# The state recurrence of a chunked linear attention: from a chain of updates to prefix scans, and a prologue with part of its constants made later

## The chip, the cores and the metric

The kernel runs on one core of a Trainium2 chip. The metric is the device time of one execution in microseconds (us), from the first to the last instruction and what lies around them. A core has five engines with an instruction queue each: the matrix engine (PE), the vector engine (DVE), the scalar engine (ACT), GpSimd (POOL) and SyncE (SP, which here only issues DMA transfers). Each engine works its own queue in order, and semaphores hold an instruction until what it needs is there.

## The reference, cut to what matters

The program is two layers of a hybrid network over 1152 tokens (128 of a prompt, 1024 of a sample; the two groups are independent sequences). In each layer a normalised and modulated input is projected to 2336 columns, which feed a windowed attention with a sink, a gated linear attention (GLA), and a gated linear recurrence (RG-LRU); an output projection and a feed-forward block of width 4096 follow. The GLA has four heads of width 64 and two directions, and works in chunks of 64 tokens:

```
b = jnp.cumsum(g, axis=2)                    # within a chunk
q_in = q * jnp.exp(b);  k_in = k * jnp.exp(-b);  k_end = k * jnp.exp(b_last - b)
o_intra = causal(q_in k_in^T) v
delta = jnp.einsum('bnchd,bnchv->bnhdv', k_end, v)
decay = jnp.exp(b_last[:, :, 0])
s[c + 1] = decay[c][:, None] * s[c] + delta[c]      # over the chunks
o = o_intra + q_in s[c]
```

So a state of 64 x 64 numbers runs over 2 chunks of the prompt (from zero) and over 16 of the sample (from a given state), forwards, and in the other direction backwards. The final states of the prompt are outputs.

## The kernel before

Every array is held with channels on the partitions and 1152 tokens along the free dimension, in three blocks (`tb`) of 384 tokens. A product in full precision is three products of split numbers (`dense`, L155 to L157), twelve of which make a tick.

PE's order is written out by hand: `tick` advances generators that sit in `self.chain`, one step for every twelve projection products, so that small PE work is strewn between the projections. The other engines get their order from a scheduler that goes by its own cost estimates and the order in the program.

**The GLA, `gla_pair`.** Two heads make a pair; a layer has two pairs. A head has its forward direction on partitions 0 to 63 and its backward direction on 64 to 127. `cum` makes the running sums of the gate (two scans over half the partitions each, L595 and L596). Then come six steps (two heads, three blocks). `pre` of a step subtracts the running sum from its value at the chunk's end (L634 on DVE for the forward half, L635 on POOL for the backward half), takes the exponential (L636, ACT) and multiplies the key (L637, DVE); `trans` transposes this on PE (L643) and copies it out (L645, ACT); `delta`, one step later, multiplies it with the values (L653, PE), copies the six 64 x 64 results out of PSUM (L654, ACT) and makes the scaled queries and keys with two exponentials (L659, L662, ACT) and two products (L660, L663, POOL). After a head's third block `states` runs the recurrence: 34 instructions `upd` (L672, DVE), one for each chunk and direction, each over 64 partitions and 64 columns. A generator spreads them over the following ticks. The states land in `Sc`, chunk by chunk.

Then `intra` multiplies queries with keys (L718), masks (L720) and adds the directions (L724); `outer` adds the contributions of values (L732) and states (L738) in one PSUM bank; `headsum` and `gate` normalise and gate the output.

**The prologue.** `run` loads and transposes the inputs, sums their squares, and makes each token's scale. While the modulation matrix streams in (`mod_round`, L249), `scaled` multiplies the three blocks with the scale (`spread`, L329, and L369, half on POOL and half on DVE). When the modulation is there (`mod_fin`, L257 to L282, which yields the gains G), `norm1_first` finishes each block: gain and shift (L380 on ACT, L382 on DVE), the high part (L383, ACT), the low part (L385). `vecs` makes the constants of a layer; its last 27 DVE instructions (L198 to L222) serve the RG-LRU and the gate alone.

Of the kernel before, what the change touches and what calls it, by code (L numbers as in the profile page):

```python
# [28 lines left out]
PPOS = 11  # L29
V_BMOD, V_N1, V_N2, V_CW, V_CB, V_GN, V_BA, V_BX, V_LAM, V_SL, V_GB, V_FN, V_C, V_CC = (  # L30
# [8 lines left out]
def blk(t, tb):  # L39
    return t[:, tb * TB:(tb + 1) * TB]  # L40
# [8 lines left out]
class Net:  # L49
# [111 lines left out]
    def vecs(self, l):  # L161
# [25 lines left out]
        if l == 0:  # L187
# [7 lines left out]
            self.cs = cs  # L195
        hb = self.const.tile([128, 8], F32, name=f"hb{l}")
# [160 lines left out]
    def scaled(self, tb, rs):  # L357
        nc = self.nc
        g = self.spread(rs, lambda: self.np.tile([128, TB], F32, tag="pb", name="pb", bufs=3))
# [6 lines left out]
        for kt, path in enumerate('pvpvpvpv'):  # L366
            t = self.np.tile([128, TB], F32, tag="nt", name="nt", bufs=24)
            eng = nc.gpsimd if path == "p" else nc.vector
            eng.tensor_tensor(t, self.xa(kt, tb), pbs, ALU.mult)  # L369
            ts.append(t)  # L370
        return ts

    def norm1_first(self, tb, ts):
# [12 lines left out]
        self.spill(tb)  # L386
        yield
# [42 lines left out]
    def mixer(self, l):  # L430
# [131 lines left out]
        def gla_pair(pair, hook):  # L562
# [49 lines left out]
            def start(hf):  # L612
                Bt, qd, kd = H[hf]
                Bc = Bt.rearrange("p (c s) -> p c s", s=64)
                dec = gp.tile([128, 18], F32, tag="dec", name="dec", bufs=2)
                nc.scalar.activation(dec[0:64], Bc[0:64, :, 63], AF.Exp, scale=-1.0 / 16)
                nc.scalar.activation(dec[64:128], Bc[64:128, :, 0], AF.Exp, scale=-1.0 / 16)
                dl, S = B(), B()
                Sc = S.rearrange("p (c v) -> p c v", v=64)
                nc.gpsimd.memset(Sc[0:64, 0], 0.0)  # L620
                nc.gpsimd.memset(Sc[64:128, 1], 0.0)
                nc.sync.dma_start(Sc[0:64, 2], I["state_gla"][0, l, 0, 2 * pair + hf])
                nc.sync.dma_start(Sc[64:128, 17], I["state_gla"][0, l, 1, 2 * pair + hf])
                st[hf] = (dec, dl, Sc, B())

            def pre(hf, tb):
# [3 lines left out]
                Bc = Bt.rearrange("p (c s) -> p c s", s=64)  # L630
# [16 lines left out]

            def delta(hf, tb, kn):
                Bt, qd, kd = H[hf]
                dec, dl, Sc, kin = st[hf]  # L650
# [6 lines left out]
                b = blk(Bt, tb)  # L657
                e = tg()
                nc.scalar.activation(e, b, AF.Exp, scale=-1.0 / 16)  # L659
                nc.gpsimd.tensor_tensor(blk(qd, tb), blk(qd, tb), e, ALU.mult)  # L660
                e = tg()
                nc.scalar.activation(e, b, AF.Exp, scale=1.0 / 16)  # L662
                nc.gpsimd.tensor_tensor(blk(kin, tb), blk(kd, tb), e, ALU.mult)  # L663

            def states(hf):
                dec, dl, Sc, kin = st[hf]
# [860 lines left out]
```

## Time and profile before

| | us |
|---|---|
| median of 3 runs (2927.18 to 2929.66) | 2928.68 |
| the profiled execution, its own time | 2926.49 |
| span of the profiled execution | 2924.7 |

The span is what the trace covers. A share in a window is busy time over its length. PEclk is the clock that PE was granted, as a share of 2.4 GHz. "Idle before" names what ended an engine's idle time.

### The profile page before, as it was taken

What the parts mean: (1) busy time and instruction counts of PE and PEld (TensorE: products, weight loads), DVE (VectorE), ACT (ScalarE), POOL (GpSimd) and SP (SyncE); (2) the same over time, 40 slices, a digit from 0 to 9 for tenths busy, and PEclk for the clock granted to TensorE, in tenths of its full rate; (3) what the DMA queues carried; (4) which work ended last, traced back from release to release, by engine and by line L of the source; (5) the groups of instructions that cost most, each with busy time, mean ns of one, the idle gap of its engine ahead of it and who ended that gap; (6) DMA issues with size and microseconds to landing.
All of it is one profiled execution on the core that took longest, in us unless ns stands there. A gap on an engine that the chain in (4) does not pass through costs nothing.

```text
span 2924.7 us, 41719 instructions
## 1 busy us (share of the span) xinstructions
PE 2749.6 (94%) x16067; PEld 2621.1 (90%) x16067; DVE 1540.2 (53%) x2818; ACT 1062.2 (36%) x1957; POOL 807.7 (28%) x843
## 2 busy tenths in 40 slices
PE   5897988999999999999987989899899999999998
PEld 3787987889999999999987879888899999999998
DVE  7668577785332333233478577777832332233235
ACT  4424447764112112211354325477622112211223
POOL 5323446752001001100223234576311001100112
PEclk7998999999999999999999999999999999999999
DMA  7535338421321111111333643662211111111113
GB/s 261 134 106 156 113 127 265 143 73 58 101 80 44 44 44 37 44 44 44 107 105 88 175 131 101 200 218 75 70 46 44 44 37 43 44 44 44 40 41 130
DMA packets 279303, 273.66 MB, mean 94 GB/s; under 512 B 30032, under 2 KB 259008, under 8 KB 279104
## 3 DMA queue, kind: packets, MB, share of 16 engines
q1 hardware_dynamic: 278888, 270.92, 30.3%
q8 instruction: 127, 2.08, 0.3%
q14 instruction: 72, 0.59, 0.1%
q10 hardware_dynamic: 216, 0.06, 0.0%
HBM read 227.02 MB, written 43.91 MB: 93 GB/s over the span
## 4 chain that ended last, share of the span: by engine, by line
PE 63%; DVE 7%; ACT 2%; issue 2%; POOL 1%; DMA 1%; SPq 0%; POOLq 0%; DVEq 0%; ACTq 0%
PE pg L156 18%; PE pg L155 18%; PE pg L157 18%; DVE B L672 1%; PE pd L155 1%; PE pg L1098 1%; PE pd L156 1%; PE pd L157 1%; PE pg L1066 1%; DVE tn L343 1%; PE pe L249 1%; PE pd L1204 1%; PE pd L1205 1%; PE pd L1206 1%; PE pg L1089 1%
## 5 line engine op out<-in xcount | busy, mean ns | idle before, releaser
L118 ACT CAST wh<-wr 128x1024 fp32r<-128x1024 f32 x228 | 239.0, 1048 | 918.2 <-PE pg L156 826.1
L156 PE MATMUL pg<-hl,wh 128*128 128x384 f32 x1584 | 538.4, 340 | 2.6 <-DVE hl L345 1.5
L155 PE MATMUL pg<-hh,wh 128*128 128x384 f32 x1584 | 538.6, 340 | 1.8 <-ACT hh L344 1.8
L157 PE MATMUL pg<-hh,wl 128*128 128x384 f32 x1584 | 536.9, 339 | 0.0
L1247 POOL TENSOR_TENSOR te<-te 128x384 f32<-128x384 f32 x192 | 166.5, 867 | 1330.3 <-ACT uh L1246 1329.4
L155 PE MATMUL pg<-uh,wh 128*128 128x384 f32 x1536 | 515.1, 335 | 0.6 <-ACT wh L118 0.6
L157 PE MATMUL pg<-uh,wl 128*128 128x384 f32 x1536 | 514.1, 335 | 1.7 <-DVE wl L119 1.7
L156 PE MATMUL pg<-ul,wh 128*128 128x384 f32 x1536 | 513.8, 334 | 0.0
L1269 DVE SCALAR_TENSOR_TENSOR x<-pg,mod,x 128x384 f32<-128x384 f32 (+2 forms) x512 | 254.3, 515 | 396.3 <-PE pg L157 396.2
L119 DVE TENSOR_TENSOR wl<-wr,wh 128x1024 fp32r<-128x1024 f32 x196 | 244.9, 1250 | 191.1 <-ACT wh L118 190.9
L1248 DVE TENSOR_TENSOR ul<-te,uh 128x384 fp32r<-128x384 f32 x192 | 107.1, 558 | 451.1 <-POOL te L1247 451.1
L155 PE MATMUL pd<-hh,wh 128*128 128x384 f32 x816 | 295.1, 362 | 25.1 <-DVE te L480 9.5
L155 PEld LDWEIGHTS pg<-hh,wh 128*128 128x128 f32 x1584 | 299.2, 189 | 5.4 <-issue 3.4
L156 PEld LDWEIGHTS pg<-hl,wh 128*128 128x128 f32 x1584 | 299.3, 189 | 5.0 <-DVE hl L351 2.4
L157 PEld LDWEIGHTS pg<-hh,wl 128*128 128x128 f32 x1584 | 299.2, 189 | 0.0
L155 PEld LDWEIGHTS pg<-uh,wh 128*128 128x128 f32 x1536 | 288.9, 188 | 4.3 <-issue 1.7
L157 PEld LDWEIGHTS pg<-uh,wl 128*128 128x128 f32 x1536 | 288.7, 188 | 2.1 <-DVE wl L119 2.0
L156 PEld LDWEIGHTS pg<-ul,wh 128*128 128x128 f32 x1536 | 288.9, 188 | 0.0
L156 PE MATMUL pd<-hl,wh 128*128 128x384 f32 x816 | 283.9, 348 | 3.3 <-DVE hl L385 3.3
L157 PE MATMUL pd<-hh,wl 128*128 128x384 f32 x816 | 283.3, 347 | 0.0
L1245 ACT ACTIVATE te<-pg 128x384 f32<-128x384 f32 x192 | 93.8, 489 | 357.7 <-PE pg L157 357.7
L155 PEld LDWEIGHTS pd<-hh,wh 128*128 128x128 f32 x816 | 160.9, 197 | 34.7 <-DVE te L480 10.8
(273 smaller groups left out, 4373.3 us busy)
## 6 DMA issues: line engine op xcount, KB each, us to landing
wr<-in_w_mlp_dram SPq DMA_DIRECT2D x144, 512.0 KB
wm<-in_w_mod_dram SPq DMA_DIRECT2D x96, 512.0 KB
wr<-in_w_out_dram SPq DMA_DIRECT2D x48, 512.0 KB
wr<-in_w_in_dram SPq DMA_DIRECT2D x36, 512.0 KB
xd<-x SPq DMA_DIRECT2D x48, 192.0 KB
x<-xd SPq DMA_DIRECT2D x48, 192.0 KB
raw<-mixd SPq DMA_DIRECT2D x40, 192.0 KB
B<-gkd SPq DMA_DIRECT2D x16, 288.0 KB
```

The costliest lines, as they stand in the source:

```text
L118: nc.scalar.copy(hi[:, :m], raw[:, :m])
L119: lo_eng.tensor_tensor(lo[:, :m], raw[:, :m], f32(hi[:, :m]), ALU.subtract)
L155: mm(out, wh[i], xs[i][0], start=i == 0, stop=False)
L156: mm(out, wh[i], xs[i][1], start=False, stop=False)
L157: mm(out, wl[i], xs[i][0], start=False, stop=i == n - 1)
L249: nc.tensor.matmul(p[32 * g:32 * g + 32, :], self.cs[:, kt, :], ws[g // 2][:, 512 * (g % 2):512 * (g % 2) + 512], start=kt == 0, stop=kt = ...
L343: nc.vector.scalar_tensor_tensor(t[:, a:b], x(kt, tb)[:, a:b], G()[:, kt, s:s + 1], pbs[:, a:b], ALU.mult, ALU.mult)
L672: nc.vector.scalar_tensor_tensor(out, Sc[r, c], dec[r, c:c + 1], dc[r, c], ALU.mult, ALU.add)
L1245: nc.scalar.activation(r, p[:, :TB], AF.Relu)
L1247: nc.gpsimd.tensor_tensor(r, r, r, ALU.mult)
L1248: nc.vector.tensor_tensor(blk(ul, tb), r, f32(blk(uh, tb)), ALU.subtract)
L1269: nc.vector.scalar_tensor_tensor(xa, p[:, a:b], self.M[l]["g2"][:, dt, s:s + 1], xa, ALU.mult, ALU.add)
```

## The change

The recurrence of a head becomes four prefix scans. A new tile `dl` holds, for each of the 64 value columns, a row of NP = 19 places: a zero, the two chunks of the prompt, the start state, and the chunks of the sample (the backward direction in reverse order, so that both directions run the same way). The decays lie in a row of the same 19 places, with zeros at the places where a new sequence starts, and are repeated 16 times (`dr`), so that one scan over 304 numbers does 16 value columns. `delta` writes its results into this order, at a step of 19 numbers, with one copy for each direction (in the first block, which has both sequences, two for each). `states` runs the scans in place, and four copies, two on ACT and two on POOL, bring the states back into chunk order in `Sc`. `pre` uses the copied chunk-end values `bl` for both directions, in one DVE instruction. There is one `dl` for all heads; `dec` has one buffer. Temporaries move from `tg` (8 to 5 buffers) to `tn` (6).

In the prologue only two blocks go through `scaled` and `norm1_first`. The third goes through the ordinary `norm`, in pieces during the first projections, and the 27 late constants are made behind it (`vecs_late`).

```diff
+NP = 19
...
+        if l:
+            self.vecs_late(l)
+
+    def vecs_late(self, l):
+        nc, V = self.nc, self.V[l]
+        vt = V["vt"]
         hb = self.const.tile([128, 8], F32, name=f"hb{l}")
...
-        g = self.spread(rs, lambda: self.np.tile([128, TB], F32, tag="pb", name="pb", bufs=3))
+        g = self.spread(rs, lambda: self.np.tile([128, TB], F32, tag="pb", name="pb", bufs=2))
...
-            t = self.np.tile([128, TB], F32, tag="nt", name="nt", bufs=24)
+            t = self.np.tile([128, TB], F32, tag="nt", name="nt", bufs=16)
...
+    def late(self, l):
+        self.vecs_late(l)
         yield
...
             def start(hf):
                 Bt, qd, kd = H[hf]
                 Bc = Bt.rearrange("p (c s) -> p c s", s=64)
-                dec = gp.tile([128, 18], F32, tag="dec", name="dec", bufs=2)
-                nc.scalar.activation(dec[0:64], Bc[0:64, :, 63], AF.Exp, scale=-1.0 / 16)
-                nc.scalar.activation(dec[64:128], Bc[64:128, :, 0], AF.Exp, scale=-1.0 / 16)
-                dl, S = B(), B()
-                Sc = S.rearrange("p (c v) -> p c v", v=64)
-                nc.gpsimd.memset(Sc[0:64, 0], 0.0)
-                nc.gpsimd.memset(Sc[64:128, 1], 0.0)
-                nc.sync.dma_start(Sc[0:64, 2], I["state_gla"][0, l, 0, 2 * pair + hf])
-                nc.sync.dma_start(Sc[64:128, 17], I["state_gla"][0, l, 1, 2 * pair + hf])
-                st[hf] = (dec, dl, Sc, B())
+                dec = gp.tile([128, NP], F32, tag="dec", name="dec", bufs=1)
+                nc.gpsimd.memset(dec, 0.0)
+                bl = gp.tile([128, 18], F32, tag="bl", name="bl", bufs=2)
+                nc.scalar.copy(bl[0:64], Bc[0:64, :, 63])
+                nc.scalar.copy(bl[64:128], Bc[64:128, :, 0])
+                for r, e, o in ((slice(0, 64), 1, (slice(1, 3), slice(4, 19))), (slice(64, 128), 0, (slice(2, 0, -1), slice(18, 3, -1)))):
+                    cs = (slice(0, 2), slice(2, 17) if e else slice(3, 18))
+                    for c, d in zip(cs, o):
+                        nc.scalar.activation(dec[r, d], bl[r, c], AF.Exp, scale=-1.0 / 16)
+                s0 = gp.tile([128, 64], F32, tag="fin", name="s0", bufs=2)
+                for d in range(2):
+                    nc.sync.dma_start(s0[64 * d:64 * d + 64], I["state_gla"][0, l, d, 2 * pair + hf])
+                dr = self.tn()[:, :16 * NP]
+                nc.gpsimd.tensor_copy(dr.rearrange("p (v s) -> p v s", s=NP), dec.unsqueeze(1).to_broadcast([128, 16, NP]))
+                st[hf] = (dr, s0, B().rearrange("p (c v) -> p c v", v=64), B(), bl)
...
-                e = tg()
-                ec = e.rearrange("p (c s) -> p c s", s=64)
-                cs = slice(6 * tb, 6 * tb + 6)
-                nc.vector.tensor_tensor(ec[0:64], Bc[0:64, cs], Bc[0:64, cs, 63:64].to_broadcast([64, 6, 64]), ALU.subtract)
-                nc.gpsimd.tensor_tensor(ec[64:128], Bc[64:128, cs], Bc[64:128, cs, 0:1].to_broadcast([64, 6, 64]), ALU.subtract)
+                e = self.tn()
+                nc.vector.tensor_tensor(e.rearrange("p (c s) -> p c s", s=64), blk(Bt, tb).rearrange("p (c s) -> p c s", s=64),
+                                        st[hf][4][:, 6 * tb:6 * tb + 6].unsqueeze(2).to_broadcast([128, 6, 64]), ALU.subtract)
...
+            dlv = dl.rearrange("p (v s) -> p s v", s=NP)
+
             def delta(hf, tb, kn):
...
-                nc.scalar.copy(blk(dl, tb), ps[:, :TB])
+                pc = ps[:, :TB].rearrange("p (c v) -> p c v", v=64)
+                if tb == 0:
+                    nc.gpsimd.tensor_copy(dlv[:, 3], st[hf][1])
+                    fs, bs = ((0, 2, 1), (2, 6, 2)), ((0, 2, 2), (3, 6, 21))
+                else:
+                    c0 = 6 * tb
+                    fs, bs = ((c0, min(c0 + 6, 17), 2),), ((c0, c0 + 6, 21),)
+                for a, b, o in fs:
+                    nc.scalar.copy(dlv[0:64, a + o:b + o], pc[0:64, a - 6 * tb:b - 6 * tb])
+                for a, b, o in bs:
+                    nc.scalar.copy(dlv[64:128, o - b + 1:o - a + 1], pc[64:128, a - 6 * tb:b - 6 * tb][:, ::-1])
...
             def states(hf):
-                dec, dl, Sc, kin = st[hf]
+                dr, s0, Sc = st[hf][:3]
                 h = 2 * pair + hf
-                dc = dl.rearrange("p (c v) -> p c v", v=64)
+                n = 16 * NP
+                for q in range(4):
+                    v = dl[:, n * q:n * q + n]
+                    nc.vector.tensor_tensor_scan(v, dr, v, 0.0, ALU.mult, ALU.add)
                 fin = gp.tile([128, 64], F32, tag="fin", name="fin", bufs=2)
-
-                def upd(out, r, c):
-                    nc.vector.scalar_tensor_tensor(out, Sc[r, c], dec[r, c:c + 1], dc[r, c], ALU.mult, ALU.add)
-
+                nc.gpsimd.tensor_copy(fin, dlv[:, 2])
...
-                upd(Sc[f, 1], f, 0)
-                upd(Sc[b, 0], b, 1)
-                for i in range(15):
-                    if i in (4, 9):
-                        yield
-                    upd(Sc[f, 3 + i], f, 2 + i)
-                    upd(Sc[b, 16 - i], b, 17 - i)
-                upd(fin[f], f, 1)
-                upd(fin[b], b, 0)
...
+                nc.scalar.copy(Sc[b, 2:18], dlv[b, 3:19][:, ::-1])
+                nc.gpsimd.tensor_copy(Sc[f, 2:18], dlv[f, 3:19])
+                nc.scalar.copy(Sc[b, 0:2], dlv[b, 0:2][:, ::-1])
+                nc.gpsimd.tensor_copy(Sc[f, 0:2], dlv[f, 0:2])
...
-        tg = lambda dt=F32: gp.tile([128, TB], dt, tag="tg", name="tg", bufs=8)
+        tg = lambda dt=F32: gp.tile([128, TB], dt, tag="tg", name="tg", bufs=5)
+        dl = gp.tile([128, 64 * NP], F32, name="dl")
+        nc.gpsimd.memset(dl.rearrange("p (v s) -> p s v", s=NP)[:, 0], 0.0)
...
-        for tb in range(NTB):
+        for tb in range(2):
             ts.append(self.scaled(tb, rs[tb]))
-            for _ in range((4, 2, KD)[tb]):
+            for _ in range((4, KD)[tb]):
                 next(mod, None)
...
-        self.N1 = [self.norm1_first(tb, ts[tb]) for tb in range(NTB)]
+        self.N1 = [self.norm1_first(tb, ts[tb]) for tb in range(2)] + [self.norm1_tb(0, 2, rs), self.late(0)]
```

## Rows read from the trace of the kernel before

**Rows 1.** The page, part 1: busy time, share and instructions of PE and others.
```profile
PE 2749.6 (94%) x16067; PEld 2621.1 (90%) x16067; DVE 1540.2 (53%) x2818; ACT 1062.2 (36%) x1957; POOL 807.7 (28%) x843
```
**Rows 2.** Windows by stage: stretch and length, busy time by engine, clock, DMA.
```profile
core 0: us, PE busy (x) PEld busy (x) DVE busy (x) ACT busy (x) POOL busy (x), PEclk, DMA share, GB/s
...
720.00:1440.00 720.00, 720.00 (x4135) 711.26 (x4134) 229.84 (x378) 145.33 (x231) 74.73 (x86) 1.00 0.18 55
```
**Rows 3.** Windows of the four GLA loops: the first, the last, the sum.
```profile
129.60:161.70 32.10, 22.10 (x129) 20.82 (x127) 29.27 (x52) 14.65 (x33) 15.29 (x17) 0.89 0.39 100
...
1668.30:1702.70 34.40, 22.08 (x135) 19.77 (x136) 30.13 (x52) 15.57 (x36) 14.95 (x18) 0.90 0.50 138
sum 133.90, PE 92.25 PEld 84.89 DVE 114.22 ACT 60.96 POOL 60.14; mean PE 23.06 PEld 21.22 DVE 28.56 ACT 15.24 POOL 15.03
```
**Rows 4.** The same four windows, instructions of L672 alone, the sum.
```profile
sum 133.90, DVE 67.57; mean DVE 16.89
```
**Rows 5.** Windows behind the four loops: the second, and the sum of four.
```profile
272.50:300.00 27.50, 24.02 (x167) 20.34 (x165) 21.33 (x50) 4.44 (x9) 3.88 (x6) 0.88 0.48 145
...
sum 85.90, PE 75.03 PEld 64.84 DVE 71.25 ACT 13.64 POOL 9.86; mean PE 18.76 PEld 16.21 DVE 17.81 ACT 3.41 POOL 2.47
```
**Rows 6.** Waits of PE: waiter, releaser, us in total, times, longest.
```profile
PE pg L643 <- DVE tg L637: 43.8, 17, 6.8
...
PE pg L732 <- DVE tg L724: 8.4, 4, 3.5
```
**Rows 7.** Timeline of the last loop, DVE and PE, and L732 in the first pair.
```profile
1687.37 6.06 DVE L672 SCALAR_TENSOR_TENSOR B<-B,dec 64x64 f32<-64x64 f32 x11
...
1696.84 0.56 DVE L637 TENSOR_TENSOR tg<-B,tg 128x384 f32<-128x384 f32 x1
...
1674.33 0.55 PE L643 MATMUL pg<-ident,tg 128*128 128x128 f32 x3 [3.11 <-DVE tg L637]
...
1697.55 0.88 PE L643 MATMUL pg<-ident,tg 128*128 128x128 f32 x3 [6.78 <-DVE tg L637]
...
174.68 0.43 PE L732 MATMUL pg<-tg,B 128*64 128x128 f32 x2
```
**Rows 8.** Single lines of the program: count, duration in ns (min/median/max), first and last start.
```profile
L672 DVE SCALAR_TENSOR_TENSOR B<-B,dec x256: 268/284/1089, 137.0 to 1714.9; 64x64 f32<-64x64 f32 x128
...
L634 DVE TENSOR_TENSOR tg<-G x24: 542/544/2857, 121.6 to 1695.0; 64x384 f32<-64x384 f32 x24
...
L635 POOL TENSOR_TENSOR tg<-G x24: 823/1022/3074, 123.5 to 1688.3; 64x384 f32<-64x384 f32 x24
...
L654 ACT COPY B<-pg x24: 459/473/513, 136.4 to 1702.9; 128x384 f32<-128x384 f32 x24
...
L617 ACT ACTIVATE dec<-G x8: 229/230/232, 121.0 to 1671.4; 64x18 f32<-64x18 f32 x8
...
L878 DVE TENSOR_TENSOR_SCAN B<-B x8: 406/573/1034, 366.3 to 1841.6; 128x128 f32<-128x128 f32 x8
L878 DVE TENSOR_TENSOR_SCAN B<-B,vt x8: 2314/2320/3029, 366.7 to 1842.3; 128x1024 f32<-128x1024 f32 x8
...
L928 POOL MEMSET smask<- x2: 185/322/458, 82.1 to 1519.6; 128x18 bf16 x2
```
**Rows 9.** Timeline of the prologue, POOL, DVE and PE.
```profile
36.43 14.64 POOL L369 TENSOR_TENSOR nt<-x,pb 128x384 f32<-128x384 f32 x12 [0.42 <-ACT pb L331]
...
44.22 8.20 DVE L369 TENSOR_TENSOR nt<-x,pb 128x384 f32<-128x384 f32 x8
52.34 0.41 DVE L257 COPY mrow<-pd 128x256 f32<-128x256 f32 x1
...
44.44 0.52 PE L329 MATMUL pe<-ident,pb 128*128 128x128 f32 x3 [2.40 <-DVE pb L324]
44.89 4.48 PE L249 MATMUL pd<-wm,cs 128*32 128x512 f32 x24
...
75.75 0.69 PE L155 MATMUL pd<-hh,wh 128*128 128x384 f32 x1 [4.54 <-ACT te L487]
```
**Rows 10.** Window behind the prologue.
```profile
76.00:95.00 19.00, 19.00 (x103) 18.89 (x104) 5.13 (x11) 3.69 (x9) 5.58 (x7) 0.92 0.51 145
```

More of the change, by code (lines that the diff above doesn't have):

```diff
@@ L386, in norm1_first @@
         self.spill(tb)
+        yield
+    def late(self, l):
+        self.vecs_late(l)
         yield
@@ L661, in delta @@
-                e = tg()
-                nc.scalar.activation(e, b, AF.Exp, scale=1.0 / 16)
-                nc.gpsimd.tensor_tensor(blk(kin, tb), blk(kd, tb), e, ALU.mult)
+                for sg, dst, src in ((-1, qd, qd), (1, st[hf][3], kd)):
+                    e = self.tn()
+                    nc.scalar.activation(e, blk(Bt, tb), AF.Exp, scale=sg / 16)
+                    nc.gpsimd.tensor_tensor(blk(dst, tb), blk(src, tb), e, ALU.mult)
             def states(hf):
-                dec, dl, Sc, kin = st[hf]
+                dr, s0, Sc = st[hf][:3]
@@ L674, in states @@
+                for d in range(2):
+                    nc.sync.dma_start(O["new_state_gla"][0, l, d, h], fin[64 * d:64 * d + 64])
                 f, b = slice(0, 64), slice(64, 128)
-                upd(Sc[f, 1], f, 0)
-                upd(Sc[b, 0], b, 1)
-                for i in range(15):
-                    if i in (4, 9):
-                        yield
-                    upd(Sc[f, 3 + i], f, 2 + i)
-                    upd(Sc[b, 16 - i], b, 17 - i)
-                upd(fin[f], f, 1)
-                upd(fin[b], b, 0)
@@ L691, in gla_pair @@
             prev = None
-            sg = iter(())
             for n in range(len(steps) + 1):
                 cur = None
-                next(sg, None)
                 if n < 2:
@@ L704, in gla_pair @@
                     if prev[1] == NTB - 1:
-                        sg = states(prev[0])
-                        next(sg)
+                        states(prev[0])
                 prev = cur
@@ L741, in outer @@
                 nc.scalar.copy(oT, po[:, :TB])
-                sq = tg()
+                sq = self.tn()
                 nc.scalar.activation(sq, oT, AF.Square)
@@ L753, in headsum @@
                 nc.gpsimd.tensor_tensor(rs, ms, self.nhalf[:, :6], ALU.pow)
-                bc = tg()
+                bc = self.tn()
                 nc.vector.tensor_copy(bc.rearrange("p (j c) -> p j c", c=64), rs.unsqueeze(2).to_broadcast([128, 6, 64]))
@@ L761, in gate @@
                     nc.tensor.transpose(pb[:, 128 * j:128 * j + 128], bc[:, 128 * j:128 * j + 128], self.ident)
-                sr = tg()
+                sr = self.tn()
                 nc.sync.dma_start(sr, blk(self.grd[pair], tb))
@@ L770, in gla_pair @@
                 As[hf] = intra(0, hf)
-                next(sg, None)
                 yield
@@ L849, in lru_all @@
                         self.dense(pi[:, :TB], [lwh[:, 2 + d]], [lwl[:, 2 + d]], [xs])
-                        r = tg()
+                        r = self.tn()
                         nc.scalar.activation(r, pr[:, :TB], AF.Tanh, bias=self.V[l]["hb"][:, j:j + 1], scale=0.5)
@@ L853, in lru_all @@
                         nc.scalar.activation(blk(s2[d], tb), r, AF.Tanh, bias=self.V[l]["sp"][:, 0, j:j + 1], scale=self.V[l]["sp"][:, 0, j:j + 1])
[L854 removed]
+                        a2 = self.tn()
                         nc.gpsimd.tensor_tensor(a2, blk(a[d], tb), blk(a[d], tb), ALU.mult)
                         nc.vector.scalar_tensor_tensor(blk(s2[d], tb), a2, 1.0, blk(s2[d], tb), ALU.add, ALU.mult)
[L857 removed]
+                        i = self.tn()
                         nc.scalar.activation(i, pi[:, :TB], AF.Tanh, bias=self.V[l]["hb"][:, 4 + j:5 + j], scale=0.5)
```

11 lines of the change are left out of this document (1 added, 10 removed).

## The prediction

> **What bounds the kernel now.** I read the page first, for the shares of the engines and the 40 slices; then the windows by stage, to see where the matrix engine (PE) is not busy; then PE's own waits, for what ends them; then the instruction order on the engine named there; last the durations of single operations. On the page PE is busy for 94% of the span [rows 1], so only its idle 175 us and the time at a lowered clock can be won. None of either lies in the long feed-forward stretches: from 720 to 1440 us PE is busy without a break at the full granted clock [rows 2]. The linear attention is different. It runs four times (two layers, two head pairs). I call the stretch from a pair's first transposition (L643) to its last delta product (L653) its loop. In the four loops, together 133.9 us, PE is busy 92.25 us and idle 41.65, at a granted clock of 0.86 to 0.90, while the vector engine (DVE) is busy 114.2 us, 85% [rows 3]. Over half of that, 67.6 us, is the line that is to go, L672 [rows 4]. The waits agree: PE waited 43.8 us for the product of L637, by far its longest entry [rows 6]. In the order of the last loop one sees why: eleven L672 hold DVE for 6.06 us, more come behind them, and PE idles 6.78 us until L637 has run [rows 7].
>
> So the loops are bound by DVE, and what DVE does there is the recurrence. Behind each loop the stretch until the first output products loses 10.9 us of PE in 85.9 us [rows 5], mostly L732 waiting for L724 (8.4 us, [rows 6]), which stands behind the second head's recurrence.
>
> **Part 1: what leaves DVE.** A head has 34 updates L672, 272 in all, 0.284 us each when alone and up to 1.09 [rows 8]. Four scans over 304 numbers replace them. The existing scans give the price: 0.406 us for 128 and 2.314 for 1024 columns, 2.13 ns a column, so 0.78 us for 304 and 3.1 us a head [rows 8]. In the loops stands one head of each pair: 67.6 us go, 12.4 come, and DVE falls from 114.2 to about 59. POOL loses L635 (24 times, 0.82 us or more [rows 8]), because one DVE instruction now does both halves at the length of L634. POOL's copies of the decay, the start state and the end state are 304 and 64 numbers; by L635's 2.1 ns a number at most 0.65 and 0.14 us, off PE's path, and what hides them is the step between two transpositions.
>
> **Part 2: what comes to ACT.** One copy of 384 columns (L654, 0.473 us) becomes two over half the partitions, and four in a head's first step. With 0.230 us for 18 and 0.473 for 384 columns [rows 8] a copy costs 0.22 us + 0.67 ns a column. The copies of a head then take 1.35 + 0.95 + 0.90 = 3.2 us where three took 1.42: 3.6 us more a pair. Six small operations at 0.23 replace two: 0.9 us for the head that starts inside the loop. Copying half of the states back is 1024 and 128 columns, 0.90 + 0.30 = 1.2 us. Together 5.7 us a pair, 22.8 in the four loops, and ACT rises from 60.96 [rows 3] to 83.8 us.
>
> **Part 3: how long the loops get.** PE's work: the granted clock averages 0.885 over the loops, so 23% of 133.9 us, 30.8 us, ran at the lower level (1.2 instead of 2.4 GHz). Half of that is lost, less the idle share of 31%: 10.6 us. That leaves 92.25 - 10.6 = 81.6 us of PE at full clock. The first wait of each loop stays: the gate's cumulative scans hold DVE in front of it, and the change leaves them alone (3.11 us in the last loop [rows 7]; the others are 2.38, 3.10 and 1.21, together 9.8); with 1.2 us of clock they make a floor of 92.6 us. Against it ACT would be 90% busy, so ACT is the next bound. An in-order engine that waits for PE and DVE in turn will not reach 90%; DVE as the bound reached 85%, and I take the same: 83.8/0.85 = 98.6 us, 35.3 less than now.
>
> **Part 4: the new wait.** All heads share one tile for the deltas. The second head's first ACT copies must wait until the first head's states have been copied out: four scans (3.1 us), about 1 us for a POOL product that holds them, then POOL's end state, and 1024 + 128 strided numbers. Such a copy is not in the trace. Lower bound: L635's 0.823 us for 384, so 2.2 us for 1024. Upper bound: the strided memset L928, 18 numbers in 0.185 us (10 ns each, 10.5 us), at worst 0.458 (25 ns, 26 us) [rows 8]. I take 2.2, the row with the same type, partitions and an SBUF read. The copies then end 6.8 us after the first head's last delta, a step is 81.6/24 = 3.4 us, so ACT stands up to 3.4 us, and behind it the copy (L645) and exponential (L636) of the next steps. PE needs those a step later; I take 1.5 us a pair, 6 in all (bounds 0 and 14). Loops: 35.3 - 6 = 29 us won.
>
> The row shows DVE operations with two SBUF inputs held up while POOL computes: L634 takes 0.542 us alone and 2.857 at most, in front of a long POOL sum [rows 8]. [...]
>
> **Part 5: behind the loops.** L732's 8.4 us and about 1 us of smaller waits vanish, as the second head's 34 updates (up to 12 us of DVE) become 3.1 us of scans and 3 us of copies. What hides these is PE's work until L732, which starts at 174.68 us in the first pair, 13 us behind its loop's end [rows 3, 7]; without it they would cost their 6 us in each pair. The lowered clock in the two longer stretches (0.88 in [rows 5]) gives back about 4. Less 2 for new work on POOL: 11 us (bounds 5 and 15).
>
> **Part 6: the prologue.** From 36.4 us POOL and DVE share the 24 products L369; POOL's 12 take 14.64 us, and DVE's last eight with their waits 8.20 [rows 9]. Only then comes the copy L257 (52.34) for the modulation, whose products PE had ended at 49.4 us [rows 9]. With the third block's eight products gone, POOL ends a third, 4.9 us, earlier; the 27 small operations of the late constants, that sat between, also leave. PE no longer waits 2.40 us for the third broadcast [rows 9]. I take 6 us earlier gains. At 75.75 PE waits 4.54 us for an evacuation L487, late on ACT behind the casts of the second and third block [rows 9]; the third block now comes in pieces behind the projections, which returns some 3 us. Against it: the third norm needs about 9 us of DVE, 1 to 2 more than before, now directly ahead of its use. 8 us won (bounds 3 and 12). The late constants land where DVE has 5.1 of 19 us to do [rows 10]; uncovered they would cost the 7 us that they take between other work now. The eight spills of the third block move behind its norm; the SP queue has nothing but four loads there, and nobody reads them until the output projection. The other buffer counts (tg 8 to 5, nt, pb) I cost at nothing: the temporaries move to six tn buffers, of which two hold decays.
>
> **The sum.** 29 + 11 + 8 = 48 us off the profiled execution's 2926.5 (span 2924.7): 2878.5. The median of the runs is 2.2 higher, so 2880.
>
> **Rivals.**
> (a) *No new bound.* ACT keeps pace and the floor is reached: 41.3 + 13 + 12 = 66 us, 2862. For it: ACT's exponentials are not needed at once. Against: 90% busy in order.
> (b) *ACT takes DVE's place.* Writing and reading at a step of 76 bytes costs ACT twice per column: 2176 numbers of deltas and 1152 of states a head, 3.7 us more a pair, 98.6 us in the loops, at 85% 116. Then 18 - 6 + 9 + 5 = 26 us: 2903. Against it: ACT's 18 numbers at 256 bytes apart took 0.230 us [rows 8], no visible surcharge. [...]
> (c) *Slower: POOL's transposing copy.* At c ns a number it holds ACT's queue for 1.024c - 2.4 us beyond a step in each pair. At L928's 10 ns this takes 32 of 54 us: 2907. From about 15 ns the whole gain is gone; at its worst 25 ns it costs 93 us: 2968. Against: L635 moves 384 in 0.823 us. [...]
> (d) *No change:* the gains of the loops are given back in waits for buffers or weights: 2928. Against: the loops use a third to a half of the DMA engines [rows 3].
>
> **How the numbers follow.** Forecast (28 to 62 us won) 0.58, (a) 0.12, (b) with the milder (c) 0.16, (d) 0.05, slower by (c) 0.09. A difference below 0.2%, 5.9 us, can't be told from none. Faster 0.86, same 0.05, slower 0.09. The range 2854 to 2916 holds the forecast, nearly all of (a) and most of (b), about 8 in 10.
>
> **What would show it.** In the profile after: L672 gone, 32 scans of about 0.8 us; DVE in the loops under two thirds busy, ACT near 85%; PE's waits for L637 down from 43.8 to about 15, the first of each loop left; L732 without a wait; loops of about 26 us; G ready near 48 us. It is wrong if POOL's copy of 1024 takes over 5 us, if ACT's half copies take 0.8, or if PE waits on L645 for as long as it did on L637.

## The result and the profile after

The changed kernel runs in 2909.65 us (median of 4 runs, 2908.05 to 2915.22) against 2929.17 for the kernel before beside it: ratio 0.9936, 95% interval 0.9918 to 0.9953. It is faster, by 19 us of the 48 that were forecast. The profiled execution took 2908.05 us, span 2906.2. Lines have moved: L643 is now L656 (transposition), L645 L658, L653 L667, L637 L650, L654 L676 (forward) and L678 (backward), L718 L731, L720 L733, L724 L737, L732 L745. The scans are L692; L698 (ACT) and L699 (POOL) bring 1024 state numbers each back into chunk order.

The page of the changed kernel, part 1, answers to [rows 1]:

```profile
PE 2748.9 (95%) x16067; PEld 2625.6 (90%) x16067; DVE 1455.2 (50%) x2577; ACT 1119.6 (39%) x2046; POOL 802.5 (28%) x848
```

DVE lost 85 us, ACT gained 57. The four loops, windows as in [rows 3]:

```profile
129.30:156.10 26.80, 20.88 (x131) 20.22 (x129) 12.99 (x16) 23.30 (x46) 17.00 (x18) 0.94 0.40 99
...
1653.40:1682.70 29.30, 21.26 (x137) 19.03 (x138) 15.24 (x19) 23.57 (x45) 16.98 (x17) 1.00 0.66 180
sum 114.50, PE 88.17 PEld 81.64 DVE 55.83 ACT 93.61 POOL 66.78; mean PE 22.04 PEld 20.41 DVE 13.96 ACT 23.40 POOL 16.69
```

DVE is busy for 49% where it had 85%, and ACT for 82% where it had 46%: by busy time the bound has passed to ACT. The run `dldve` below shows that busy time is not all of it. The same four windows, only what touches the tile of deltas:

```profile
sum 114.50, DVE 15.93 ACT 43.22 POOL 12.67; mean DVE 3.98 ACT 10.80 POOL 3.17
```

Nearly half of ACT's time is copies into and out of this tile. Groups of one line and shape (busy us, mean ns; then idle before):

```profile
L698 ACT COPY B<-dl 64x1024 f32<-64x1024 f32 x8 | 17.7, 2208 | 15.4 <-DVE dl L692 15.4
L678 ACT COPY dl<-pg 64x384 f32<-64x384 f32 x16 | 14.6, 912 | 0.2
...
L678 ACT COPY dl<-pg 64x128 f32<-64x128 f32 x8 | 3.2, 404 | 0.1
...
L699 POOL COPY B<-dl 64x1024 f32<-64x1024 f32 x8 | 17.6, 2197 | 0.0
L692 DVE TENSOR_TENSOR_SCAN dl<-tn,dl 128x304 f32<-128x304 f32 x32 | 27.3, 913 | 31.6 <-issue 17.0 <-ACT dl L678 14.5
```

A copy of 384 numbers takes 0.912 us, not 0.47 to 0.48, and one of 1024 takes 2.21, not 0.90: 2.0 ns a number between 128 and 384. The numbers that follow each other in such a copy lie 76 bytes apart in the tile, 19 places of 4 bytes; this is called the step below. PE's waits, answering to [rows 6]:

```profile
PE pg L667 <- ACT tg L658: 13.7, 8, 4.8
PE pe L313 <- DVE tn L306: 13.3, 6, 3.0
PE pg L656 <- DVE tn L650: 12.2, 4, 4.5
PE pd L156 <- DVE te L491: 11.1, 3, 5.3
...
PE pg L745 <- DVE tg L737: 8.0, 2, 4.0
```

The 43.8 us for DVE's product are down to 12.2, but 13.7 for ACT's L658 are new, and L745 (before: L732) still waits 8.0. Where the time came from and went is plainest from the start of the same PE product in both traces (us; lead = before less after):

```
                                   before   after   lead
first product of the gate's input    94.9    91.2    3.6
pair 1  first transposition         129.6   129.3    0.3
        last delta                  161.1   154.9    6.1
        second block's L731         179.7   171.4    8.3
pair 2  first transposition         236.8   230.5    6.3
        last delta                  271.8   258.7   13.1
        second block's L731         295.0   275.6   19.4
        third block's L731          310.1   298.4   11.7
layer 2, pair 1  first transp.     1560.5  1548.0   12.6
        last delta                 1591.6  1575.8   15.8
        second block's L731        1611.1  1594.3   16.8
pair 2  first transposition        1668.3  1653.4   14.9
        last delta                 1702.0  1681.5   20.5
        second block's L731        1725.2  1698.4   26.8
        third block's L731         1740.3  1721.3   19.0
end of the span                    2924.7  2906.2   18.5
```

A loop here runs from the first transposition to the last delta. The loops won 5.8 + 6.8 + 3.2 + 5.6 = 21.4 us (forecast 29). Behind them, until the second block, 2.2 + 6.3 + 1.0 + 6.3 = 15.8 were won (forecast 11), and the second pairs then gave back 7.7 and 7.8. The prologue's 3.6 (forecast 8) was down to 0.3 before the first loop; 3.5 went elsewhere.

This loss of 15.5 us is called the give-back below. From the timeline of the last pair:

```profile
1688.61 2.20 POOL L699 COPY B<-dl 64x1024 f32<-64x1024 f32 x1
1690.76 0.42 POOL L701 COPY B<-dl 64x128 f32<-64x128 f32 x1
1691.13 0.52 POOL L803 MEMSET B<- 128x512 f32 x1
...
1694.67 1.26 SPq L806 DMA_DIRECT2D B<-in_lru_wx_dram  x2
...
1701.16 0.62 ACT L811 CAST B<-B 128x512 fp32r<-128x512 f32 x1 [5.24 <-issue]
...
1701.81 0.69 DVE L812 TENSOR_TENSOR B<-B 128x512 fp32r<-128x512 f32 x1 [5.02 <-ACT B L811]
1702.54 0.88 DVE L823 TENSOR_SCALAR B<-B,vt 128x1152 f32<-128x1152 f32 x1
1703.45 1.54 DVE L827 SCALAR_TENSOR_TENSOR B<-B,vt 128x126 f32<-128x126 f32 x2
...
1713.38 0.56 DVE L530 SCALAR_TENSOR_TENSOR te<-te 128x384 f32<-128x384 f32 x1 [1.44 <-ACT te L529]
...
1714.90 0.56 DVE L737 TENSOR_TENSOR tg<-tg,tn 128x384 f32<-128x384 f32 x1
...
1715.52 0.48 PE L745 MATMUL pg<-tg,B 128*64 128x128 f32 x1 [3.99 <-DVE tg L737]
```

DVE, free of the updates, is now given the RG-LRU's input convolution (L823, L827) and its weights ahead of the masks. POOL clears the weights' tile only behind its copies of the states. The first half of the load then goes out at 1691.67, and the second, behind a store and two other loads in SP's queue, at 1694.67. ACT's cast L811 stands 5.24 us, and DVE's L812 behind it. The profile names no releaser for this cast, but for the same one in the first layer it names the load:

```profile
278.54 0.62 ACT L811 CAST B<-B 128x512 fp32r<-128x512 f32 x1 [5.42 <-DMA B<-in_lru_wx_dram]
```

The masks, the head sums and L737 come late behind the convolution, and PE waits 3.99 us and runs at the lower clock after it (granted 0.50 from 1716 to 1720 us, 1.00 from 1720 to 1725; products of 384 columns start every 0.32 us at the one and every 0.175 at the other). In the kernel before:

```profile
1717.55 0.87 DVE L811 TENSOR_SCALAR B<-B,vt 128x1152 f32<-128x1152 f32 x1
1718.33 0.55 DVE L724 TENSOR_TENSOR tg<-tg 128x384 f32<-128x384 f32 x1
1718.80 4.45 DVE L815 SCALAR_TENSOR_TENSOR B<-B,vt 128x126 f32<-128x126 f32 x6
```

There too the convolution's first step (L811) ran ahead of L724, but 7.6 us before PE's first product of the second block (1725.2); in the changed kernel the same step begins some 4 us behind that product (1698.4). So what is new is less the order than the lateness.

And the loss ahead of the first loop. The kernel before, DVE, POOL and PE:

```profile
118.39 2.56 DVE L596 TENSOR_TENSOR_SCAN G<-smask,G 64x1152 f32<-64x1152 bf16 x1
...
118.42 4.98 POOL L594 TENSOR_TENSOR G<-G,B 128x1152 f32<-128x1152 f32 x1 [35.91 <-DVE G L595]
...
121.59 0.44 PE L155 MATMUL pd<-hh,wh 128*128 128x384 f32 x1 [2.89 <-DVE te L480]
```

The changed kernel:

```profile
114.73 5.01 DVE L607 TENSOR_TENSOR_SCAN G<-smask,G 64x1152 f32<-64x1152 bf16 x1
...
114.71 2.61 POOL L605 TENSOR_TENSOR G<-G,B 128x1152 f32<-128x1152 f32 x1 [30.37 <-DVE G L606]
...
120.39 0.69 PE L156 MATMUL pd<-hh,wh 128*128 128x384 f32 x1 [5.32 <-DVE te L491]
```

Before, DVE's scan began 30 ns ahead and took 2.56 us, and POOL's sum was held (4.98 us); now POOL begins 20 ns ahead, its sum takes 2.61 us, and the scan is held for nearly the length of the sum (5.01 us, 2.45 more than before), and PE waits 2.43 us more, most of the 3.3 us of lead that are lost here.

### The profile page after: what moved, and what is told of

It reads as the page before. It is cut to its first block, busy times and chain, and to the rows that moved or that the text cites. A ratio compares the mean times of both kernels' runs of the same rounds, so it can differ in the third digit from the quotient of the medians.

```text
span 2906.2 us, 41527 instructions
## 1 busy us (share of the span) xinstructions
PE 2748.9 (95%) x16067; PEld 2625.6 (90%) x16067; DVE 1455.2 (50%) x2577; ACT 1119.6 (39%) x2046; POOL 802.5 (28%) x848
## 3 DMA queue, kind: packets, MB, share of 16 engines
q1 hardware_dynamic: 278888, 270.92, 30.5%
```

## The experiments

Two theories were tried. Theory 1: ACT pays for the step of 76 bytes, and as the bound of the loops it ate the gain. Theory 2: ACT's order and the wait on the one tile count, not its busy time. Beside them stood the prologue, the gate's scans and the convolution. After each time stand its ratio and the 95% interval. Each ratio is against the kernel before on the same chip, and "better" is the distance to that kernel's median less the change's 19.5 us; loops: the sum, over four, from first transposition to last delta (before 131.2 us, changed 109.8). An interval reaches 3 to 6 us to either side, so by the times alone a gain under some 7 us on the changed kernel can't be told from none, nor two runs that lie so close.

**The two halves alone.** `gla_only` has the prologue of before, `pro_only` the recurrence of before.

> The scans of the change with the prologue of before. If the whole gain is the recurrence's (my reading of the two traces: the prologue's lead of 3.6 us at the gate's product is back to 0.3 us when the first loop begins), this runs in 2909 to 2912 us, as the changed kernel does. If the prologue is worth what I forecast for it, 8 us, it runs in 2917 us or more.

> The prologue of the change with the 34 updates a head of before. My reading: 2926 to 2929 us (0 to 3 us better than before), because the earlier start meets the gate's cumulative scans. Rival, my forecast: 2921 us.

Measured: 2918.76 (0.9968, 0.9956 to 0.9979) and 2922.21 us (0.9985, 0.9974 to 0.9995): 10.0 and 6.5 us below the 2928.76 beside them. My reading fell: alone, the prologue is worth nearly what was forecast. Its lead is still 4.7 us at the first loop and 3.8 at 1740 us, since in `pro_only` the scan began 40 ns ahead of POOL's sum and took 2.55 us. In `gla_only` POOL began 30 ns ahead, the scan was held for 5.00 us, and the first loop began 4.5 us later than before. So the held scan comes with the recurrence's part and not with the prologue's earlier start.

**Deltas without a step.**

```diff
-dlv = dl.rearrange("p (v s) -> p s v", s=NP)
+dlv = dl.rearrange("p (s v) -> p s v", v=64)
```

> As the changed kernel, but the deltas lie place by place (64 numbers next to each other) instead of column by column at a step of 19 numbers. The scans run over numbers in the wrong order, with the same count and form, so the output is not the reference's. Theory 1, the step of 76 bytes is what ACT pays for and ACT bounds the loops: the copies of 384 columns fall from 0.91 to about 0.48 us, the copy of 1024 from 2.2 to about 0.9, ACT in the four loops from 94 to about 73 us, and the kernel gains 8 to 14 us on the changed one (2896 to 2902). Theory 2, ACT's order and its waits bound the loops and not its busy time: under 4 us gained. If the copies stay at 0.9 us, it is the half of the partitions or PSUM that costs, not the step.

Measured: 2877.76 us (0.9832, 0.9818 to 0.9846), 31.5 better than the change, far more than the 8 to 14 that theory 1 expected. Its groups:

```profile
L698 ACT COPY B<-dl 64x1024 f32<-64x1024 f32 x8 | 8.4, 1045 | 7.8 <-DVE dl L692 5.5 <-POOL B L701 2.3
L678 ACT COPY dl<-pg 64x384 f32<-64x384 f32 x16 | 7.6, 474 | 0.3
...
L678 ACT COPY dl<-pg 64x128 f32<-64x128 f32 x8 | 2.1, 261 | 0.1
...
L699 POOL COPY B<-dl 64x1024 f32<-64x1024 f32 x8 | 8.3, 1035 | 0.9 <-DVE dl L692 0.7
```

Same instructions, partitions and counts, half the time: the step costs, on ACT and on POOL. Loops: 95.6 us, 14.2 less than in the change, just above what theory 1 expected of the whole. The rest is mostly the give-back, which is gone too (third block 15.1 us behind the second, as before the change; 22.8 and 23.0 with it): with POOL's copies at 1.04 us the second half of the weights' load was issued 7.6 us behind the last delta and not 13.2, and the convolution began 5.0 us ahead of the second block's first product. The order the scheduler chose there differs as well.

The four loops of `contig`, each window ending 1.0 to 1.3 us behind the start of the last delta, as in the change:

```profile
sum 100.20, PE 86.95 PEld 81.39 DVE 55.23 ACT 76.76 POOL 63.37; mean PE 21.74 PEld 20.35 DVE 13.81 ACT 19.19 POOL 15.84
```

**Which side of a copy pays.** In `inner` the copies go column by column:

```diff
-nc.scalar.copy(dlv[0:64, a + o:b + o], pc[0:64, a - 6 * tb:b - 6 * tb])
+nc.scalar.copy(dlv[0:64, a + o:b + o].rearrange("p s v -> p v s"), pc[0:64, a - 6 * tb:b - 6 * tb].rearrange("p c v -> p v c"))
```

and likewise L678, L698, L699. In `scfast` only the states' copies lose the step, on their read side:

```diff
 f, b = slice(0, 64), slice(64, 128)
+dlv = dl.rearrange("p (s v) -> p s v", v=64)
 nc.scalar.copy(Sc[b, 2:18], dlv[b, 3:19][:, ::-1])
```

> As the changed kernel, but each of the copies of the deltas and of the 1024 state numbers goes through its numbers column by column (the places inside), so that six or sixteen neighbouring numbers of the shared tile follow each other; the other side, PSUM or the states in chunk order, is then reached at a step of 256 bytes. It tells whether reading or writing at a step costs. If a step on the written side costs: the copies of 384 fall from 0.91 to about 0.5 us, the copies of 1024 stay near 2.2, and 4 to 8 us are gained on the changed kernel's 2909. If a step on the read side costs: the copies of 1024 fall to about 1.05 us and those of 384 stay or rise. If any step on either side costs, nothing is gained.

> As the changed kernel, deltas and scans untouched, but the four copies of the states read the shared tile place by place, 64 neighbouring numbers at a time, and no longer at a step of 19 numbers. The states are then the wrong numbers, in the same count, so the output is not the reference's. It shares out the 32 us by which the contiguous kernel beat the changed one: the delta copies written without a step gave 15.7 of them (with the states' copies hardly faster). If the rest belongs to the states' copies, between the two heads of a pair, this gains about 12 to 18 us on the changed kernel's 2909 (2891 to 2897), with copies of 1024 at 1.05 us on ACT and POOL. If ACT's busy time alone counts, it gains only what the copies leave: 8 times 1.2 us, half of it in the loops, 4 to 6 us.

Measured: 2893.38 (0.9866, 0.9849 to 0.9883) and 2897.65 us (0.9889, 0.9874 to 0.9904). The groups of `inner`:

```profile
L698 ACT COPY B<-dl 64x1024 f32<-64x1024 f32 x8 | 16.2, 2024 | 14.2 <-DVE dl L692 14.2
L678 ACT COPY dl<-pg 64x384 f32<-64x384 f32 x16 | 8.2, 515 | 0.2
...
L678 ACT COPY dl<-pg 64x128 f32<-64x128 f32 x8 | 2.4, 299 | 0.1
```

PSUM read at a step of 256 bytes costs next to nothing (0.515 against 0.474), and runs of six numbers in the tile are written nearly at full pace. SBUF at a step costs on either side: the 1024 read in runs but written at 256 bytes still take 2.02. `inner` is 17.7 better, far more than the 4 to 8 expected, and `scfast` 12.8, together 30.5 of `contig`'s 31.5. The 12.8 are more than the 9.3 us of busy time that ACT's copies of the states lose, but not by more than the noise; that theory 2 has its share is likely, since L698 stood 15.4 us for the scans with the next head's copies behind it, and not shown. Only 3.5 and 4.0 us of these gains lie in the loops (106.3 and 105.8 us), 7.5 of the 14.2 that `contig` won there with both. Either edit also cuts the two give-backs of 7.7, to between 3 and 5.4, and in both the convolution begins 1.4 to 2.1 us behind the second block's first product: later than in `contig`, where nothing is given back, and earlier than in the change.

**ACT relieved another way.** The backward delta copies on DVE.

```diff
-nc.scalar.copy(dlv[64:128, o - b + 1:o - a + 1], pc[64:128, a - 6 * tb:b - 6 * tb][:, ::-1])
+nc.vector.tensor_copy(dlv[64:128, o - b + 1:o - a + 1], pc[64:128, a - 6 * tb:b - 6 * tb][:, ::-1])
```

> As the changed kernel, but the backward half of the delta copies (24 of 48 long ones and 8 short ones) runs on DVE. Theory 1, ACT is the loops' bound: ACT loses about 21 us of the 94 that it is busy in the four loops, DVE (56 busy in 114) has room for it, and 4 to 10 us are gained on the changed kernel (2899 to 2905), less if the step costs DVE as much as ACT (0.9 us each) since DVE's queue then stands in front of the subtractions. Rival: the order and the waits count and not ACT's load: within 3 us of the changed kernel.

Measured: 2901.13 us (0.9896, 0.9876 to 0.9916), 9.9 better, in the range that theory 1 gave, but not in its place. ACT's busy time in the loops fell to 75.1 us, and the loops became only 2.4 us shorter (107.4), while PE's wait for ACT's L658 grew (four windows taken in the same way, and the wait):

```profile
sum 112.30, PE 88.20 PEld 82.58 DVE 69.84 ACT 75.11 POOL 63.13; mean PE 22.05 PEld 20.65 DVE 17.46 ACT 18.78 POOL 15.78
...
PE pg L667 <- ACT tg L658: 16.8, 7, 4.6
```

So the loops' length doesn't follow ACT's busy time alone. DVE pays the step as well, against L524, a copy out of PSUM without a step:

```profile
L678 DVE COPY dl<-pg 64x384 f32<-64x384 f32 x16 | 14.7, 921 | 8.6 <-ACT dl L676 8.5
...
L524 DVE COPY te<-pd 128x384 f32<-128x384 f32 x12 | 6.7, 554 | 5.2 <-PE pd L158 5.1
```

**The convolution held back**, by the second block's head sums times zero.

```diff
-nc.gpsimd.memset(lw, 0.0)
+nc.gpsimd.tensor_scalar(lw[:, 0:3], self.fence.rearrange("p (a c) -> p a c", a=3), 0.0, None, ALU.mult)
+nc.gpsimd.memset(lw[:, 3], 0.0)
...
+nc.vector.scalar_tensor_tensor(w2, self.fence[:, :1], 0.0, w(2), ALU.mult, ALU.add)
-nc.vector.tensor_scalar(xc, lx, w(2), vt[:, V_CB + t:V_CB + t + 1], ALU.mult, ALU.add)
+nc.vector.tensor_scalar(xc, lx, w2, vt[:, V_CB + t:V_CB + t + 1], ALU.mult, ALU.add)
```

> As the changed kernel, but the convolution of the RG-LRU's input and the load of its gate weights are held, by a false dependence, until the second pair's second block has its head sums. Theory: in the second pair of each layer the cast of these weights stood on ACT, and their low part on DVE, 5.2 us for the load, and the convolution then stood in front of the mask, so that the lead over the kernel before fell from 19.4 to 11.7 us and from 26.8 to 19.0 us at the second output product. Then this gains 10 to 15 us on the changed kernel (2895 to 2900). Rival: DVE's convolution is only moved to another place on PE's path, and the time stays within 4 us of the changed kernel's 2909.

Measured: 2901.08 us (0.9911, 0.9899 to 0.9923), 8.2 better, less than the theory. The third block follows the second after 15.1 us in both second pairs: the give-back of 15.5 is gone. But the loops took 116.0 us, 6.2 more than in the changed kernel; why was not settled (other orders of the queues).

**The second head's gate sum on DVE.**

```diff
-eng = nc.gpsimd if hf else nc.vector
-eng.tensor_tensor(Bt, Bt, mns[hf], ALU.subtract)
+nc.vector.tensor_tensor(Bt, Bt, mns[hf], ALU.subtract)
```

> As the changed kernel, but the second head's sum of the gate runs on DVE and not on POOL. Theory: in the changed kernel POOL's sum began 20 ns ahead of DVE's second cumulative scan in the first pair of each layer and held it from 2.55 to 5.0 us, PE waited 5.3 us behind it instead of 2.9; on DVE the sum takes 1.36 us. Then PE's wait falls to about 2.9 us or, if the sum is put ahead of the evacuation, 4.2, and 2 to 5 us are gained. Rival: the sum's 1.36 us on DVE cost as much as they give, within 1.5 us of the changed kernel.

Measured: 2906.76 us (0.9914, 0.9899 to 0.9929), 4.3 better, which the times alone can't tell from none; the traces show what moved. PE's wait is 2.88 us again and the first loop begins 3.6 us earlier, but ends only 1.8 earlier; the loops took 119.2 us.

**The late constants tied to the third norm.** In the changed kernel they were still made early, between DVE's products:

```profile
43.85 0.98 DVE L222 TENSOR_SCALAR s4b<-s4b 128x4 f32<-128x4 f32 x1
44.86 0.92 DVE L221 TENSOR_TENSOR s4b<-s4b,s 128x4 f32<-128x4 f32 x1
...
47.62 1.95 DVE L376 TENSOR_TENSOR nt<-x,pb 128x384 f32<-128x384 f32 x4
...
50.62 0.41 DVE L264 COPY mrow<-pd 128x256 f32<-128x256 f32 x1
...
52.03 0.25 DVE L289 SCALAR_TENSOR_TENSOR G<-mod,vt 128x8 f32<-128x8 f32 x2
```

```diff
+vt = self.const.tile([128, 14], F32, name="vtl")
+nc.vector.scalar_tensor_tensor(vt, f32(self.hl1[7])[:, T - 14:], 0.0, V["vt"][:, V_GN:V_GN + 14], ALU.mult, ALU.add)
```

In `latef2` the first line is `vt = self.small(16, "s16")[:, :14]`.

> As the changed kernel, but the late constants of the first layer are tied, by a false dependence, to the end of the third norm, so that they can't run earlier. Theory: in the changed kernel they still ran at 31 to 51 us, in front of the copy for the modulation, because the scheduler took them as soon as DVE was free; tied, the gains G are ready 2 to 4 us earlier (52.3 to about 49), and up to 3 us of it reach the end. Rival: DVE's products and POOL set G and not the constants; then G moves by less than 1 us and the time by none.

> As the kernel with the late constants tied to the third norm, but their tied input lies in a tile that is there anyway, so that no address moves. The tied kernel began its first loop 1.9 us ahead of the changed one and lost 5.5 us in the first feed-forward part, where PE waited for nothing and did 3177 products in 560 us instead of 3208. If the moved addresses did that, this one has 3208 there and runs in 2905 to 2908 us, up to 3 better than the changed kernel. If not, the slow part is there again, and the time is near 2918.

Measured: 2918.38 us (0.9955, 0.9940 to 0.9971) with a new tile, 7.3 worse than the change, and 2906.06 (0.9928, 0.9910 to 0.9945) with an old one, 4.4 better. Only the 12 us between the two stand clear of the noise. In `latef2`:

```profile
46.09 0.41 DVE L269 COPY mrow<-pd 128x256 f32<-128x256 f32 x1
...
47.24 0.25 DVE L294 SCALAR_TENSOR_TENSOR G<-mod,vt 128x8 f32<-128x8 f32 x2
```

G is there 4.8 us earlier than in the change, and the first loop begins 4.8 earlier. The loss of `latef` lies in the feed-forward part of layer 1. Windows there, changed kernel (PE busy, count, clock):

```profile
840.00:1400.00 560.00, 560.00 (x3208) 1.00 0.15 44
```

and `latef`:

```profile
840.00:1400.00 560.00, 560.00 (x3177) 1.00 0.14 43
```

No wait, the same clock, 1% fewer products; `latef2` has 3208. The two differ in 56 bytes of allocation alone. That the moved addresses do it is the author's estimate, and no run shows by what way.

**No copies of the states at all.** In `direct` each head has its own tile, forward and backward halves are scanned apart (eight scans), and PE reads the states out of it at a step of 80 bytes. `best2` adds the three edits `hold`, `cumdve` and `latef2`.

```diff
-nc.vector.tensor_tensor_scan(v, dr, v, 0.0, ALU.mult, ALU.add)
+nc.vector.tensor_tensor_scan(v[f], dr[f], v[f], 0.0, ALU.mult, ALU.add)
+nc.vector.tensor_tensor_scan(v[b, ::-1], dr[b, ::-1], v[b, ::-1], 0.0, ALU.mult, ALU.add)
...
-B = lambda dt=F32: gp.tile([128, T], dt, tag="B", name="B", bufs=10)
+B = lambda dt=F32: gp.tile([128, T], dt, tag="B", name="B", bufs=8)
```

> The changed kernel without any copying of the states: each head has a tile of deltas of its own, the forward and the backward half are scanned apart (eight scans over 64 partitions a head, the backward ones from the end), so that the entering state of a chunk lies in the same place for both, and PE reads its states out of the scanned tile, at a step of 20 numbers. The deltas are copied column by column. What the copies of the states still cost in the column-by-column kernel (2893): 2.0 us on ACT and on POOL in each head, between the two heads, and the second head's wait for the one tile. Theory: these are what is left between 2893 and my forecast, so this gains 10 to 16 us on 2893 (2877 to 2883); DVE's four extra scans a head (3 us) have room. Rivals: PE's loads of states at a step cost PE itself (144 loads a layer pair; at 0.1 us each about 14 us, no gain); or DVE's doubled scans, held by POOL's products, take the place (2890 or more).

> The kernel without copies of the states, with the three other edits that gained: the convolution held back, the second gate sum on DVE, the late constants tied to the third norm. If they add up as in the kernel of three edits (6.9 us beside the column-by-column copies) and the tied constants give 3 more: 9 to 10 us below the kernel without copies of the states, near 2870. If PE's strided loads cost what the copies gave, it ends where the kernel of three edits does, 2884 to 2887. The product is the reference's.

Measured: 2900.77 (0.9910, 0.9894 to 0.9927) and 2887.43 us (0.9863, 0.9848 to 0.9878): both rivals came true. PE's loads of the states, in `inner`, then in `direct` (ns, min/median/max):

```profile
L751 PEld LDWEIGHTS pg<-B x288: 133/138/231, 168.6 to 1724.0; 128*64 128x64 f32 x144
```

```profile
L748 PEld LDWEIGHTS pg<-B,dl x288: 192/215/231, 169.7 to 1723.4; 128*64 128x64 f32 x144
```

From one block's L731 to the next takes PE 0.6 us more. In the first pair eight scans stand in DVE's queue for 9.3 us, four of them at 1.45 to 1.53 us where the other four took 0.81 or 0.82 (that POOL's products held them is the author's estimate: ACT waited for two of these, L683, until 143.69 and 145.16 us), and PE waited for the L650 behind them:

```profile
151.41 0.87 PE L656 MATMUL pg<-ident,tn 128*128 128x128 f32 x3 [9.41 <-DVE tn L650]
```

The other three loops took 69.3 us where `inner` has 79.4, so the states' copies and the one tile did hold them. What this won went to PE's loads and to that wait; whether the fewer buffers (`B`, 10 to 8) cost something was not tried.

**The version that beats both.** `best1` joins `inner`, `hold` and `cumdve`; `best3` adds `latef2`.

> The changed kernel with three edits together: copies that go column by column through the deltas and states, the convolution and its weights held to the second pair's second block, the second head's gate sum on DVE. Singly they gained about 15.7, 8 and 2.5 us on 2909. If they add up: 2883. If the first and the second remove the same wait (the column-by-column copies already kept 2.8 and 4.8 us of the lead at the second output product), 2887 to 2891. The product is the reference's.

> The kernel of three edits (copies column by column, convolution held, second gate sum on DVE) with the late constants tied to the third norm as the fourth; the states are copied, as in the changed kernel. The tied constants alone gave 3 us on the changed kernel (2906), and began the first loop 4.8 us earlier. If they add: 2883. If what they give is lost before the first loop, because the gate sum on DVE already took that wait: 2886 to 2888, as the kernel of three edits.

Measured: 2886.48 (0.9854, 0.9839 to 0.9868) and 2883.09 us (0.9846, 0.9828 to 0.9863). By the medians `best3` is 47 us faster than the kernel before, about what was forecast for the change, but by another way: its loops take 108.6 us, hardly less than the change's 109.8. It has a lead of 7.7 us at the first loop where the change had 0.3, and no give-back.

## Why the prediction failed, step by step

**Part 1** held. L672 is gone; a scan takes 0.77 us alone and 0.91 in the mean (0.78 and holds were taken); DVE is busy 55.8 us in the loops (59).

**Part 2 is the step that failed.** It priced every copy at 0.22 us + 0.67 ns a number, from 384 numbers without a step, and took ACT's 18 numbers at 256 bytes apart in 0.230 us as proof that a step is free [rows 8]. At 18 numbers a surcharge of 1.15 ns (1.98 less 0.83, both below) is by estimate 0.02 us and hidden in the fixed part. Measured between 128 and 384 numbers, one costs 1.98 ns at the step, (912 - 404)/256, and 0.83 without, (474 - 261)/256. ACT in the loops became 93.6 us instead of 83.8. The prediction named the mark itself, half copies of 0.8 us; they took 0.91. Rival (b) had the mechanism, twice per column, and came to 2903. A copy of 384 takes 0.474 us with 64 numbers in a row (`contig`) and 0.515 with six (`inner`); one of 128 takes 0.261, and 0.299 with two. The kernel without the step runs in 2877.8 us, 2 from the forecast, and that is in part luck: its loops won 35.6 us for the 29 forecast, the stretches up to the second block 16.1 for 11, its prologue had 1.8 us of the 8 left at the first loop, and some 10 went elsewhere.

**Part 3** came out in number and not in mechanism. In the change ACT was busy 82% of the loops (85% taken), and in `contig`, near the price forecast, the loops fell by 35.6 us (35.3). But ACT was busy there for 76.8 us and not 83.8, and for 77% of the windows and not 85%; the two errors cancel, which is luck. And `dldve` relieved ACT without shortening the loops much, so that ACT's busy time divided by a fixed share does not give their length. The lower clock of the forecast, half of the full one, is in the trace of before as a share (0.50 from 1697 to 1699 us, 1.00 from 1701 to 1703); no trace gives it in GHz.

**Part 4** had POOL's copy right (2.197 us for 2.2), so (c) was not the case, but by luck: the row it was priced by, L635, has two inputs and no step, and POOL's copy without a step takes 1.035 us. The step more than doubles it. Whether the wait between the heads was sized right is not shown: `scfast`, which halves the long copies there, won 4.0 us in the loops, where 6 were charged for the whole wait.

**Part 5** had the right sign up to the second block (15.8 us for 11, just beyond the bound of 15) and missed what DVE would be given in the place of the updates: the convolution, ahead of the masks and late, since the load of its weights stands behind POOL's copies, for 15.5 us. It said that L732 would not wait; L745 waits 8.0 us, one block later.

**Part 6** had G "6 us earlier"; it came 1.7 earlier (54.0 to 52.3), since the constants did not leave: the scheduler made them as soon as DVE was free. Tied, G is 6.5 us earlier than before. L487's wait fell from 4.54 to 1.88 us, as said. That the lead can be lost ahead of the first loop, to POOL's sum that holds DVE's scan, it did not see.

So the misses are 8 us in the loops, 11 net behind them, 8 in the prologue, and 3.5 in smaller places; `contig`, where neither is there, shows that the first two hang on the step, and `hold` that the give-back hangs on the convolution. Rivals (a) and (d) were not the case.

## What to carry to other kernels

Price a copy by a row with the same step in SBUF and enough numbers to show a slope: a short row hides it (by the estimate above 0.02 us in 18 numbers). Where an order must be changed on the way from PSUM, read PSUM at the step and write SBUF in runs (here 0.515 us for 384 numbers instead of 0.912). A row of another form that gives the same price may do so by chance. When a full engine is emptied, look at what the scheduler will put there and at what will then come late: the place in the program did not move the constants here, and a false dependence did.

## What the runs showed of the hardware

- A step of 76 bytes in SBUF about doubles a copy on ACT, written (0.474 to 0.912 us for 384) or read (1.045 to 2.208 for 1024), and on POOL, read (1.035 to 2.197 for 1024). DVE, writing at it, takes 0.921 us for 384, where another copy without a step takes 0.554. PSUM read at 256 bytes, with runs of six written, costs 0.04 us in 384.
- PE's loads of weights pay too: 64 columns take 138 ns next to each other (`inner`) and 215 at 80 bytes apart (`direct`).
- Of DVE's scan and POOL's sum, the one that began 20 to 40 ns ahead ran at its own pace and the other was held, in all four traces compared: 2.56 and 4.98 us, or 5.01 and 2.61.
- A new tile of 56 bytes went with 1% fewer products in a stretch without waits (3177 for 3208 in 560 us).
